# Row softmax with a relative-position bias: a sixth chunk buffer, masks built inside it, and stores that wait on a count of scaled chunks

## Chip, cores, metric

One core of one Trainium2 chip. The metric is the device time of one execution in microseconds (us), as the median of several. The other cores of the chip ran nothing of this program.

## The reference, cut to what matters

```python
B, H, S, max_rel = 2, 8, 2112, 16
logits: [B, H, S, S] float32;  rel_bias: [H, 33] float32
rel  = clip(i - j, -16, 16) + 16          # i: row, j: column
x    = logits + rel_bias[:, rel]           # the same bias for both b
out  = softmax(x, axis=-1)                 # float32
```

285.5 MB come in and 285.5 MB go out. Each element needs one addition, one exponential, one sum and one multiplication.

## The kernel before

Each of the 128 partitions owns 264 rows. They pass in 66 chunks of 4 rows (33,792 bytes per partition and chunk, 4,224 KB per transfer). SyncE issues the loads. VectorE adds the bias, which lies as one strip `F` in on-chip memory and is read at a shifted offset. ScalarE takes the exponential and the row sums; VectorE inverts the sums and scales; ScalarE issues the store. There are `BUFS` chunk buffers, and the result of chunk n is stored when chunk n+2 has had its first half added ("lag 2"; the first five stores have lag 1).

```python
R = 4; HALF = 2; BUFS = 5; NEAR = 7
qi, mm, qm, eq, lt, gt, rest = ...         # seven small mask tiles [128, 71]
L   = [const.tile([P, R*S], FP32) for u in range(BUFS)]

def store(eng, u, start):                  # ScalarE's queue
    eng.dma_start(out=rows(out, start), in_=L[u][:]).then_inc(stored[u], 16)

def reload(eng, u, start):                 # SyncE's queue
    take(eng, stored[u], 16)               # wait and count down
    load(eng, u, start)

def exps(eng, u, first):                   # ScalarE
    for s0 in range(0, R, HALF):
        take(eng, added, 1)
        if s0 == 0:
            first()                        # issues the store of an earlier chunk
        ...                                # activation with sum, twice
        e.then_inc(summed, 1)

def vec(eng, u, start, last=False):        # VectorE
    take(eng, loaded[u], 16)
    ...                                    # two additions
    ...                                    # reciprocal, scaling, twice
    if last:
        e.then_inc(scaled, 1)              # only the last store needs it
# ... (strip construction, loops over chunks: cut)
```

The softmax here doesn't subtract the row's maximum and nothing guards it: scores larger than these inputs give would overflow.

## Time and profile before

| | before |
|---|---|
| time, 3 runs | 1330.77 us (1329.46 to 1331.22) |
| the profiled execution | 1350.82 us (span 1349.0) |
| VectorE / ScalarE busy | 71% / 39% |
| DMA queues, loads + stores | 99.6% of 16 engines' span |
| moved | 571.00 MB |

Read it from the bottom: the compute engines idle a good part of the time while both DMA queues together leave nothing over. The prediction shows those lines. One part of the page that it uses without showing is the time from issue to landing (columns: tensors, issuing queue, operation, count, KB each, median us to landing):

```profile
out_dram<-L ACTq DMA_DIRECT2D x66, 4224.0 KB, 25.3
L<-in_logits_dram SPq DMA_DIRECT2D x65, 4224.0 KB, 30.4
```

A transfer needs 10.0 us of all engines and lands after 25 to 30. The rest of that time it stands in line or shares the engines with others.

### The profile page before, as it was taken

How to read it: one execution, taken by the hardware profiler on the slowest of the kernel's cores; microseconds unless marked ns; L12 is line 12 of the kernel's file. 1: busy time of each engine (PE TensorE's matmuls, PEld its weight loads, DVE VectorE, ACT ScalarE, POOL GpSimd, SP SyncE). 2: the span in 40 equal slices, each digit the busy share in tenths (PEclk: the TensorE clock that was granted, in tenths of full speed). 3: DMA queues.
4: the chain of work that ended last, by engine and by line, in shares of the span. 5: the costliest groups of instructions: out<-in, count | busy, mean ns of one | idle time of the engine just before them, and what ended most of it. 6: DMA issues, size and time to landing. Idle time of an engine off the chain costs nothing. (4 is left out here: it accounts for less than half of the span.)

```text
span 1349.0 us, 2476 instructions
## 1 busy us (share of the span) xinstructions
DVE 960.6 (71%) x539; ACT 527.1 (39%) x529; POOL 0.5 (0%) x6
## 2 busy tenths in 40 slices
DVE  5888766766766766766767767767767767767763
ACT  2444433424424424424424424434334334334332
POOL 0000000000000000000000000000000000000000
DMA  9999999999999999999999999999999999999997
GB/s 395 424 428 433 432 431 430 430 432 430 431 424 427 426 428 424 425 420 431 424 428 419 431 429 421 428 425 430 421 430 423 430 428 419 426 422 431 424 428 318
DMA packets 19587, 571.00 MB, mean 423 GB/s; under 512 B 2304, under 2 KB 2304, under 8 KB 2304
## 3 DMA queue, kind: packets, MB, share of 16 engines
q10 hardware_dynamic: 9648, 285.50, 50.1%
q1 hardware_dynamic: 9936, 285.48, 49.5%
q14 instruction: 3, 0.02, 0.0%
HBM read 285.49 MB, written 285.47 MB: 423 GB/s over the span
## 5 line engine op out<-in xcount | busy, mean ns | idle before, releaser
L120 ACT ACTIVATE L<-L 128x2112 f32<-128x2112 f32 x264 | 516.0, 1955 | 775.8 <-ACTq L86 759.6
L111 DVE TENSOR_TENSOR L<-L,F 128x4224 f32<-128x4224 f32 x132 | 595.8, 4555 | 239.2 <-DVEq L86 239.2
L134 DVE TENSOR_SCALAR L<-L,tot 128x2112 f32<-128x2112 f32 x264 | 336.5, 1317 | 21.6 <-DVEq L86 3.9
L130 DVE RECIPROCAL tot<-tot 128x2 f32<-128x2 f32 x132 | 21.9, 166 | 97.0 <-DVEq L86 97.0
L120 ACT ACTIVATION_READ_ACCUMULATOR L<-L 128x1 f32 x264 | 49.2, 186 | 0.0
L120 ACT ACT_TABLE_LOAD x1 | 1.3, 1283 | 23.1 <-ACTq L86 23.1
L178 DVE TENSOR_SCALAR rest<-lt,rbP 128x71 f32<-128x71 f32 x1 | 0.3, 257 | 7.7 <-DVEq L86 7.7
L186 DVE TENSOR_TENSOR F<-eq,rbP 128x2343 f32<-128x2343 f32 x1 | 2.6, 2600 | 0.1
L187 DVE TENSOR_TENSOR F<-F,rest 128x2343 f32<-128x2343 f32 x1 | 2.6, 2599 | 0.1
L173 DVE TENSOR_SCALAR qi<-qi 128x71 int32<-128x71 int32 x1 | 0.2, 199 | 1.5 <-DVEq L86 1.5
L181 DVE SCALAR_TENSOR_TENSOR rest<-gt,rbP,rest 128x71 f32<-128x71 f32 x1 | 0.3, 294 | 0.2 <-DVEq L86 0.2
L174 DVE TENSOR_TENSOR qm<-qi,mm 128x71 f32<-128x71 int32 x1 | 0.2, 233 | 0.1
L176 DVE TENSOR_SCALAR lt<-qm 128x71 f32<-128x71 f32 x1 | 0.2, 199 | 0.1
L176 DVE TENSOR_SCALAR eq<-qm 128x71 f32<-128x71 f32 x1 | 0.2, 198 | 0.1
L176 DVE TENSOR_SCALAR gt<-qm 128x71 f32<-128x71 f32 x1 | 0.2, 198 | 0.1
L179 DVE COPY F<-rbP 128x16 f32<-128x16 f32 x1 | 0.2, 175 | 0.1
L185 DVE COPY F<-rbP 128x16 f32<-128x16 f32 x1 | 0.2, 175 | 0.1
L210 POOL IOTA mm<- 128x71 int32 x1 | 0.2, 188 | 0.0
L207 POOL IOTA qi<- 128x71 int32 x1 | 0.2, 187 | 0.6 <-SPq L74 0.6
L265 POOL MEMSET const-bfloat16-1.0<- 128x1 bf16 x1 | 0.1, 102 | 0.0
L265 POOL MEMSET const-uint8-127<- 128x1 uint8 x1 | 0.1, 102 | 0.0
L265 POOL MEMSET const-float32-0.0<- 128x1 f32 x1 | 0.1, 99 | 0.2 <-issue 0.2
(1 smaller groups left out, 0.1 us busy)
## 6 DMA issues: line engine op xcount, KB each, us to landing
out_dram<-L ACTq DMA_DIRECT2D x66, 4224.0 KB, 25.3
L<-in_logits_dram SPq DMA_DIRECT2D x65, 4224.0 KB, 30.4
L<-in_logits_dram SPq DMA_DIRECT2D x4, 1056.0 KB, 8.9
rbP<-in_rel_bias_dram ACTq DMA_DIRECT2D x2, 8.2 KB
```

What stands on the lines that cost most here:

```text
L111: eng.tensor_tensor(out=x3, in0=x3, in1=F3, op=ALU.add).then_inc(added, 1)
L120: e = eng.activation(out=x, in_=x, func=EXP, accum_out=tot[u][:, i : i + 1])
L130: eng.reciprocal(out=t, in_=t).then_inc(inverted, 1)
L134: e = eng.tensor_scalar_mul(out=x, in0=x, scalar1=tot[u][:, i : i + 1])
L173: step(eng.tensor_single_scalar(out=qi[:], in_=qi[:], scalar=M * Q - 1, op=ALU.bitwise_and))
L174: step(eng.tensor_tensor(out=qm[:], in0=qi[:], in1=mm[:], op=ALU.subtract))
L176: step(eng.tensor_scalar(out=m[:], in0=qm[:], scalar1=0.0, scalar2=None, op0=op))
L178: step(eng.tensor_scalar(out=rest[:], in0=lt[:], scalar1=low, scalar2=None, op0=ALU.mult))
L181: eng.scalar_tensor_tensor(out=rest[:], in0=gt[:], scalar=high, in1=rest[:], op0=ALU.mult, op1=ALU.add)
L186: step(eng.tensor_tensor(out=blocks, in0=wide(eq), in1=rev, op=ALU.mult))
L187: step(eng.tensor_tensor(out=blocks, in0=blocks, in1=wide(rest), op=ALU.add))
L265: nc = _bacc.Bacc("TRN2", target_bir_lowering=False, num_devices=1)
```

## The change

The intent: one chunk more in flight, so that VectorE waits less for loads. By the prediction's accounting six buffers and the masks do not fit in the memory together, so the masks are built inside the last buffer and its first load waits until the strip is done. Every store now also takes a count that VectorE raises after scaling a chunk.

```diff
-    BUFS = 5
+    BUFS = 6
-    NEAR = 7
+    NEAR = 4
-    qi = const.tile([P, NB], INT32, tag="qi", name="qi")
-    ... six more mask tiles ...
+    qi, mm, qm, eq, lt, gt, rest = (
+        L[BUFS - 1][:, NB * m : NB * (m + 1)] for m in range(7)
+    )
     def store(eng, u, start):
+        take(eng, scaled, 1)
         eng.dma_start(out=rows(out, start), in_=L[u][:]).then_inc(stored[u], 16)
     def vec(...):
-        if last:
-            e.then_inc(scaled, 1)
+        e.then_inc(scaled, 1)
     # end of the strip's construction
+        eng.sem_inc(made, 1)
     # SyncE, first loads
             for u in range(1, BUFS):
+                if u == BUFS - 1:
+                    take(eng, made, 1)
                 load(eng, u, u * R)
```

`NEAR` is the chunk from which the looped part of ScalarE's program runs. With 4 instead of 7, the first two stores have lag 1 instead of the first five.

More of the change, by code (lines that the diff above doesn't have):

```diff
@@ L58 @@
     rbP = const.tile([P, W], FP32, tag="rbP", name="rbP")
-    qi = const.tile([P, NB], INT32, tag="qi", name="qi")
-    mm = const.tile([P, NB], INT32, tag="mm", name="mm")
-    qm = const.tile([P, NB], FP32, tag="qm", name="qm")
-    eq = const.tile([P, NB], FP32, tag="eq", name="eq")
-    lt = const.tile([P, NB], FP32, tag="lt", name="lt")
-    gt = const.tile([P, NB], FP32, tag="gt", name="gt")
-    rest = const.tile([P, NB], FP32, tag="rest", name="rest")
     L = [const.tile([P, RS], FP32, tag=f"L{u}", name=f"L{u}") for u in range(BUFS)]
     tot = [const.tile([P, R], FP32, tag=f"tot{u}", name=f"tot{u}") for u in range(BUFS)]
+    qi, mm, qm, eq, lt, gt, rest = (
+        L[BUFS - 1][:, NB * m : NB * (m + 1)] for m in range(7)
+    )
+    qi = qi.bitcast(INT32)
+    mm = mm.bitcast(INT32)
     def rows(t, start, run=RS):
@@ L79 @@
     strip = nc.alloc_semaphore("strip")
+    made = nc.alloc_semaphore("made")
     added = nc.alloc_semaphore("added")
@@ L121, in exps, with vec @@
             e.then_inc(summed, 1)
-    def vec(eng, u, start, last=False):
+    def vec(eng, u, start):
         take(eng, loaded[u], 16)
@@ L172, in strip_of @@
         take(eng, blocks_ready, 2)
-        step(eng.tensor_single_scalar(out=qi[:], in_=qi[:], scalar=M * Q - 1, op=ALU.bitwise_and))
-        step(eng.tensor_tensor(out=qm[:], in0=qi[:], in1=mm[:], op=ALU.subtract))
+        step(eng.tensor_single_scalar(out=qi, in_=qi, scalar=M * Q - 1, op=ALU.bitwise_and))
+        step(eng.tensor_tensor(out=qm, in0=qi, in1=mm, op=ALU.subtract))
         for m, op in ((eq, ALU.is_equal), (lt, ALU.is_gt), (gt, ALU.is_lt)):
-            step(eng.tensor_scalar(out=m[:], in0=qm[:], scalar1=0.0, scalar2=None, op0=op))
+            step(eng.tensor_scalar(out=m, in0=qm, scalar1=0.0, scalar2=None, op0=op))
         take(eng, table, 16 * B)
-        step(eng.tensor_scalar(out=rest[:], in0=lt[:], scalar1=low, scalar2=None, op0=ALU.mult))
+        step(eng.tensor_scalar(out=rest, in0=lt, scalar1=low, scalar2=None, op0=ALU.mult))
         step(eng.tensor_copy(out=F[:, 0:MR], in_=low.to_broadcast([P, MR])))
@@ L181, in strip_of @@
             eng.scalar_tensor_tensor(
-                out=rest[:], in0=gt[:], scalar=high, in1=rest[:], op0=ALU.mult, op1=ALU.add
+                out=rest, in0=gt, scalar=high, in1=rest, op0=ALU.mult, op1=ALU.add
             )
@@ L206, in _ @@
         def _(eng):
-            eng.iota(qi[:], pattern=[[0, NB]], base=0, channel_multiplier=M).then_inc(
+            eng.iota(qi, pattern=[[0, NB]], base=0, channel_multiplier=M).then_inc(
                 blocks_ready, 1
             )
-            eng.iota(mm[:], pattern=[[1, NB]], base=1 - M, channel_multiplier=0).then_inc(
+            eng.iota(mm, pattern=[[1, NB]], base=1 - M, channel_multiplier=0).then_inc(
                 blocks_ready, 1
@@ L241, in _ @@
             exps(eng, (N - 1) % BUFS, out_of(N - 2))
-            take(eng, scaled, 1)
             store(eng, (N - 1) % BUFS, (N - 1) * R)
@@ L248, in _ @@
             eng.wait_ge(loaded[0], 16 * R).then_inc(loaded[0], 16 - 16 * R)
-            passes(eng, 0, N - 1, lambda u, start: vec(eng, u, start))
-            vec(eng, (N - 1) % BUFS, (N - 1) * R, last=True)
+            passes(eng, 0, N, lambda u, start: vec(eng, u, start))
 _INS = ['logits', 'rel_bias']
```

## The prediction

> **What bounds the kernel now.** I read the page first, its strip of 40 slices and its DMA parts. The engines are far from full (VectorE 71%, ScalarE 39%), the DMA row is not:
>
> ```profile
> span 1349.0 us, 2476 instructions
> DVE 960.6 (71%) x539; ACT 527.1 (39%) x529; POOL 0.5 (0%) x6
> ...
> DMA  9999999999999999999999999999999999999997
> GB/s 395 424 428 433 432 431 430 430 432 430 431 424 427 426 428 424 425 420 431 424 428 419 431 429 421 428 425 430 421 430 423 430 428 419 426 422 431 424 428 318
> q10 hardware_dynamic: 9648, 285.50, 50.1%
> q1 hardware_dynamic: 9936, 285.48, 49.5%
> ```
>
> The two queues (stores 50.1%, loads 49.5%) together fill 99.6% of the time of all 16 DMA engines. The only slices under 419 GB/s are the first and the last. Next I read the waits, because a sixth buffer is an answer to waits:
>
> ```profile
> ACT L L120 <- ACTq L86: 759.6, 65, 13.1
> DVE L L111 <- DVEq L86: 239.2, 59, 4.9
> DVE tot L130 <- DVEq L86: 97.0, 131, 3.3
> ```
>
> The second line is VectorE waiting for a loaded chunk, 59 times, 239.2 / 59 = 4.1 us each. It is the sort of idle time that another buffer seems to promise back. Whether it can depends on whether the DMA engines are idle meanwhile. They are not, as stretches of the middle and both ends show (columns: stretch, length, busy time of VectorE, ScalarE, GpSimd, clock, DMA share, GB/s):
>
> ```profile
> 0.00:2.00 2.00, 0.34 (x2) 0.00 (x0) 0.53 (x6) 1.00 0.07 13
> 2.00:4.00 2.00, 0.69 (x4) 0.00 (x0) 0.00 (x0) 1.00 0.98 279
> ...
> 360.00:380.00 20.00, 14.05 (x9) 7.97 (x8) 0.00 (x0) 1.00 1.01 431
> 380.00:400.00 20.00, 13.99 (x9) 7.97 (x8) 0.00 (x0) 1.00 0.99 419
> ...
> 1330.00:1334.00 4.00, 0.00 (x0) 0.00 (x0) 0.00 (x0) 1.00 1.20 515
> 1334.00:1338.00 4.00, 0.00 (x0) 0.00 (x0) 0.00 (x0) 1.00 0.94 406
> 1338.00:1342.00 4.00, 0.00 (x0) 0.00 (x0) 0.00 (x0) 1.00 0.41 177
> 1342.00:1346.00 4.00, 0.00 (x0) 0.00 (x0) 0.00 (x0) 1.00 0.12 51
> ```
>
> The share is 1.00 throughout, in stretches of 431 and of 419 GB/s alike. So the dips are slower packets, not idle engines. The packet records say the same: nearly always 16 packets are in flight, one per engine. Of 16,768 packets of 33,792 bytes, 15,837 took 1.24 to 1.26 us (1.251 typically) and some took up to 2.5 us.
>
> **The floor.** A chunk is 128 such packets one way: 128 x 1.251 / 16 = 10.0 us. 66 chunks in and 66 out are 132 x 10.008 = 1321 us. The first chunk comes in quarters, whose 512 small packets took 11.1 us instead of 10.0, and completion writes took 1.2 us in all: 1323.4 us of pure transfer. In the profile the packets' times add up to 1343 us per engine, so about 19.5 us are slow packets. The profiled run took 1350.82 us against 1330.77 us unprofiled, 20.05 us more. I read that as: the slow packets mostly belong to profiling, and the timed run has few. Then the timed run is 1323.4 plus about 2.2 us before the first data moves, plus what is left, 1330.77 - 1325.6 = 5 us, for the last completion, unevenness between engines at the end and a few slow packets. This 5 us is all that any buffering can reach: 0.4%.
>
> **What the Trainium skill says.** "DMA: Bandwidth & Descriptors", section "Where 436 GB/s comes from", puts the ceiling of the 16 ports at 435.2 GB/s. The trace agrees: 16 x 33,792 B / 1.251 us = 432 GB/s, and the timed run averages 571.00 MB / 1330.77 us = 429 GB/s, 98.6% of the page's figure. The same section expects HBM to bind nearer 358 GB/s; here it doesn't, and the measurement decides. "SBUF — State Buffer", section "SBUF size: 192, 224, or 256?", leaves 208 KiB (212,992 B) per partition after the scratch. Six buffers of 33,792 B, the strip of 9,500 B, the table of 132 B and six sums of 16 B are 212,480 B. The seven masks (7 x 71 x 4 = 1,988 B) would not fit beside them, which is why they move into the last buffer; no run here shows the limit itself. "DMA: Bandwidth & Descriptors", section "Anatomy of one DMA — SWDGE (gpsimd) path", says that DMA engines do not wait on semaphores, and that a wait is made by the issuing sequencer. So the new waits stop SyncE's or ScalarE's queue, not a transfer already queued. In the trace the loads already queued flow while SyncE waits 1306.8 us in all.
>
> **The change part by part.**
>
> *Sixth buffer.* It removes no byte and no packet. Now a buffer's cycle is: the add starts as the load lands; the store two chunks behind is issued 4.8 us after an add starts (1211.50 to 1216.30); so a chunk's store comes 2 periods + 4.8 us after its own add. Landing times are 25.3 us for the store and 30.4 us for the reload. With a period of about 20.3 us (adds at 1211.50 and 1231.75) that is 45.4 + 25.3 + 30.4 = 101.1 us, and 5 periods are 101.5 us. So the loop is tight. But a loop can be tight because its transfers queue: 55.7 us of landing time in a period of 20.3 us means 2.7 transfers always outstanding, each needing 10.0 us of all engines. With six buffers the cycle is 6 x 20.3 = 121.8 us, so landing times grow to 121.8 - 45.4 = 76 us together and 3.8 transfers stand in line. The period remains two chunk transfers. Gain in the steady part: 0. VectorE's wait stays near 4 us a chunk, 60 times less the few chunks for which the extra buffer keeps it fed at the start (its own period when fed is 16.2 us).
>
> *Gate on the masks.* Load of buffer 5 waits for the strip, ready at 17.7 us (last strip instruction 15.13 + 2.60). Before it 5 chunks are queued, 50 us of transfer, so the queue holds until about 52 us. Cost 0.
>
> *First stores.* Stores 0 and 1 still go one chunk behind (39.9 and 56.4 us), but store 2 now goes with chunk 4 at about 88.5 us instead of 72.4. Is there enough to move till then? At 40 us, 37.6 us of the 60 us of first loads are done. Sharing evenly, store 0 ends at about 60 us and releases a reload, store 1 at about 80 us and releases another. Supply until 88.5 us: 60 + 2 x 10 + 2 x 10 = 100 us, used 86.3. Some 14 us are in hand; idle 0.
>
> *Wait on scaled chunks.* One more semaphore wait for each of 66 stores on ScalarE's queue. The store already waits for an add that VectorE runs after that chunk's scaling, so the count is there. At an estimated 0.1 us each (the gaps between dependent VectorE steps in the strip are about 0.1 to 0.15 us) it is 6.6 us on an engine that idles 775 us before activations. On the path: 0.
>
> *The end.* Last stores are issued as before: two with chunk 64, one with 65, one after the last scaling (issued 1329.15). At the last load's landing (about 1312) two to four stores are unfinished, the engines are full past 1334, and only then thin out unevenly. A store queue one deeper could hide a little of the last chunk's 16 us of compute and even out the engines: 0 to 3 us. I take 1 us.
>
> Sum: 1330.77 - 1 = about 1329.5 us.
>
> **The rivals.** (1) *The loads' wait is real latency*, and the buffer takes away VectorE's 239 us of idling, or part: even a tenth would be 24 us, 1307 us. For it: the wait is regular and the cycle is tight to 0.4 us. Against: DMA share 1.00 and a floor of 1323.4 us that is made of bytes. (2) *Deeper queues change packet speed.* Store packets took 1.251 to 1.255 us until 240 us and 1.28 to 1.30 us later, so traffic can be slower for reasons I can't see. If the timed run got the profile's whole 19.5 us of slow packets it would be 1350 us; if only a quarter, 1335. The opposite, all vanished, is about 1327. (3) *Later stores or the gate starve the start*: if my even sharing is wrong by more than 14 us, some microseconds idle, 1332 to 1340. (4) *The extra wait delays a store* in the last, exposed chunk: 0.1 us.
>
> **Range and chances.** The low end is the floor plus start and completion, about 1325; the high end allows a fifth of rival 2 or a little of rival 3, 1334. Over 2% faster would be under 1304 us, under the floor; over 2% slower would be over 1357 us and needs a starved stage or a slow mode of the memory. Chances 0.01, 0.98, 0.01.
>
> **What would show it.** Right: DMA share 1.00 and 420 to 433 GB/s in the middle, the load's and the store's landing times together near 76 us instead of 55.7, VectorE still waiting about 4 us a chunk for loads though starting some four chunks later, the first load of buffer 5 issued at about 18 us without a gap in DMA. Wrong: packets clearly faster than 1.25 us, a slice after the first under 415 GB/s, a DMA share under 0.95 between 40 and 100 us (rival 3), or store packets much slower over the whole span (rival 2).

## More of the kernel before

The wait `take(eng, added, 1)` ahead of a store of chunk n-2 already implies that chunk n-2 is scaled: VectorE's program adds chunk n only after scaling chunk n-1, and without the added wait (e6) the result is correct.

The profiled execution is 1.6% over the fastest timed one. I took that for a cost of profiling.

## The result

The changed kernel took 1332.64 us (4 runs, 1330.96 to 1333.23) against 1330.78 us of before (4 runs): ratio 1.0014, 95% interval 0.9996 to 1.0031. Ratios here and below are the mean time of one kernel's fast runs over that of the other's fast runs of the same rounds, so not quite the ratio of the medians that I quote. Executions over 1.5% slower than the fastest of the same kernel are left out of the means. The result lies inside the predicted range (1325 to 1334), and in the class "within 2%". My expected value was 1329.5.

The profile after, first its page:

```profile
span 1331.2 us, 2545 instructions
DVE 960.4 (72%) x539; ACT 522.7 (39%) x529; POOL 0.5 (0%) x6
...
GB/s 396 426 420 425 425 434 435 430 435 437 427 436 437 427 436 436 429 435 437 429 435 437 429 436 436 429 436 437 427 436 437 430 433 438 429 434 438 429 434 337
q1 hardware_dynamic: 9936, 285.48, 49.9%
q10 hardware_dynamic: 9648, 285.50, 49.8%
```

Again the queues fill 99.7% together. Bytes and packets are the same. Next the wait that the buffer was to remove (what waited, for what; us in total, times, longest), and the landing times:

```profile
DVE L L113 <- DVEq L87: 214.7, 58, 4.2
```

```profile
out_dram<-L ACTq DMA_DIRECT2D x66, 4224.0 KB, 44.6
L<-in_logits_dram SPq DMA_DIRECT2D x65, 4224.0 KB, 29.8
```

VectorE still waits 214.7 / 58 = 3.7 us a chunk. The landing times of a store and a load together went from 55.7 to 74.4 us. The new buffer holds a chunk that stands in line to be stored. Last, stretches at the start, in the middle and at the end (stretch, length, busy time of VectorE, ScalarE, GpSimd, clock, DMA share, GB/s):

```profile
0.00:2.00 2.00, 0.34 (x2) 0.00 (x0) 0.53 (x6) 1.00 0.00 0
2.00:4.00 2.00, 0.69 (x4) 0.00 (x0) 0.00 (x0) 1.00 1.02 325
360.00:380.00 20.00, 14.46 (x8) 7.82 (x9) 0.00 (x0) 1.00 1.00 433
...
1318.00:1322.00 4.00, 0.00 (x0) 0.00 (x0) 0.00 (x0) 1.00 0.96 414
1322.00:1326.00 4.00, 0.00 (x0) 0.00 (x0) 0.00 (x0) 1.00 0.39 169
1326.00:1331.00 5.00, 0.00 (x0) 0.00 (x0) 0.00 (x0) 1.00 0.08 34
```

The middle is full at 433 GB/s. At the start 2 us pass before data flows. At the end the compute engines are done at 1301 us, and the DMA engines thin out between 1322 and 1331 us: most have finished, one or two are late. These edges, and about 3 us per engine by which packets exceed their typical 1.251 us, are all that is not transfer.

### The profile page after: what moved, and what is told of

It reads as the page before. It is cut to its first block, busy times and chain, and to the rows that moved or that the text cites. A ratio compares the mean times of both kernels' runs of the same rounds, so it can differ in the third digit from the quotient of the medians.

```text
span 1331.2 us, 2545 instructions
## 1 busy us (share of the span) xinstructions
DVE 960.4 (72%) x539; ACT 522.7 (39%) x529; POOL 0.5 (0%) x6
## 5 line engine op out<-in xcount | busy, mean ns | idle before, releaser
L113 DVE TENSOR_TENSOR L<-L,F 128x4224 f32<-128x4224 f32 x132 | 595.7, 4554 | 214.7 <-DVEq L87 214.7
## 6 DMA issues: line engine op xcount, KB each, us to landing
out_dram<-L ACTq DMA_DIRECT2D x66, 4224.0 KB, 44.6
L<-in_logits_dram SPq DMA_DIRECT2D x65, 4224.0 KB, 29.8
```

The costliest lines, as they stand in the source:

```text
L113: eng.tensor_tensor(out=x3, in0=x3, in1=F3, op=ALU.add).then_inc(added, 1)
```

## The experiments

Theory: the kernel is bound by the transfer of its bytes, and what matters of the buffers is only whether enough transfers stand in line to keep 16 engines busy. Rivals: the loads' wait is real latency; six buffers help or hurt by themselves and another part of the change hides it; slow packets come from profiling or from the buffers. Kernels e1 to e4 ran on one chip, e5 to e8 on a second, e9 and e10 on that second chip in another session, and e11 and e12 on a third, each time beside the kernel before.

### e1: the kernel before, profiled again

No edit.

> The kernel before, unchanged, profiled once more. My prediction read the profile of before (1350.82 us against 1330.77 timed, about 19.5 us of slow packets) as a cost of profiling. If that is so, this profile is again near 1350 us with 15 to 20 us of slow packets. If it was the chance of that one execution, this profile is within 5 us of its timed runs, with under 6 us of slow packets, as the profile of the changed kernel was (1332.95). Rival: if five buffers as such make slow packets, the profile is again over 1340 us while kernels with six are not. Timed: ratio 1.000 within 0.002 in each case; it gives the noise of the comparison.

Measured: 1330.51 us, ratio 0.9994 (0.9973 to 1.0015). Its profile:

```profile
span 1329.4 us, 2476 instructions
...
q1 hardware_dynamic: 9936, 285.48, 49.9%
q10 hardware_dynamic: 9648, 285.50, 49.8%
```

A profiled execution is as fast as a timed one. The packet records show about 2 us of slow packets per engine (the time by which packets of 33,792 bytes exceed 1.251 us each) where the first profile had 19.5, nearly all among the loads of the first 160 us. So my reading of the 20 us as a cost of profiling is false: executions as long also come without a profile. Three of the other executions of five- and six-buffer kernels were as long or nearly (before at 1345.92 and 1352.37, e12 at 1351.80), with five and with six buffers. The first profile of before is such a slow execution. What slows the packets in them stays open. Against this second profile, the clearest difference between before and after is in the landing times: e1 has 25.7 and 28.9 us. VectorE waits 222.1 us in 59 waits there, 3.8 us each, against 3.7 in after.

### e2: the transfers alone

```diff
 # ScalarE: no exponentials
+    def copy(u, start, n=16):
+        take(eng, loaded[u], n)
+        eng.dma_start(out=rows(out, start), in_=L[u][:]).then_inc(stored[u], 16)
+    copy(0, 0, 16 * R)
+    passes(eng, 1, N, copy)
 # VectorE: the strip only
-    passes(eng, 0, N, lambda u, start: vec(eng, u, start))
```

The result is wrong: it returns the logits.

> Six buffers, same loads and stores, but no adding, no exponentials, no scaling: a store waits only for its load (wrong result on purpose). Transfer theory: the time is that of the bytes, 1323 us plus start and unevenness of the engines at the end, so 1325 to 1332 us, within 0.4% of both kernels. Rival (the loads' wait is real latency that more buffers or faster compute could win back): well below, under 1315 us. Rival (compute at the end is exposed): 1318 to 1324 us.

Measured: 1327.11 us (1326.36 to 1327.60), ratio to before 0.9971 (0.9952 to 0.9990). With no computation at all, the same transfers take 3.4 us less than the whole kernel. So removing all the compute is worth 0.3%, or 0.5% at the interval's edge. No other order of these transfers was tried, so that it bounds every arrangement is argued. The rival that promised VectorE's 239 us back is dead: the changed kernel, run again with its compute on another chip (e11), took 1327.08 us.

### e3 and e4: four and three buffers

```diff
-    BUFS = 6
+    BUFS = 4      # e3;  3 in e4
```

> The changed kernel with four buffers. With stores two chunks behind, two periods are 4.8 us plus landing of a store plus landing of a load. Transfer theory: saturation needs 40.4 us for two periods, so landing times of together 35.6 us, 1.7 transfers in line on average; that is enough or just short: 1332 to 1375 us, DMA share 0.97 to 1.00, landing times together about 36 us. Rival (a buffer's cycle is a fixed latency of about 101 us, five buffers being just enough): cycle 101 us over four buffers is 25 us a chunk, about 1670 us.

> The changed kernel with three buffers. One period is then 4.8 us plus landing of a store plus landing of a load with nothing else in line, each 10 us of transfer plus 1 to 2 us: 27 to 29 us a chunk, 1780 to 1920 us, DMA share about 0.7. Rival (fixed cycle of 101 us): 34 us a chunk, about 2220 us.

Measured: four buffers 1557.41 us (1522.87 to 1560.93; only the fastest of the four counts as fast, so no ratio is given, and the profile is of the slowest, 1560.93 us; e10 below repeats the case with fast runs), three buffers 1912.87 us, ratio 1.4372 (1.4345 to 1.4399).

Three is as expected: the cycle of a buffer leaves one period for 4.8 us plus both landings, 4.8 + 11.4 + 12.4 = 28.6 us, and the adds are 29.2 us apart (617.08 and 646.32). Four missed my range by 180 us, and the rival's 1670 missed by 113. The rule for the cycle holds, 4.8 + 21.8 + 20.7 = 47.3 us for two periods, or 23.7 us each, 66 x 23.7 = 1564 us. What fails is my assumption that 1.7 transfers in line on average keep the engines full:

```profile
q1 hardware_dynamic: 9936, 285.48, 48.3%
q10 hardware_dynamic: 9648, 285.50, 42.5%
```

```profile
640.00:650.00 10.00, 2.05 (x2) 0.00 (x0) 0.00 (x0) 1.00 1.00 433
650.00:660.00 10.00, 9.14 (x3) 4.26 (x5) 0.00 (x0) 1.00 0.77 280
660.00:670.00 10.00, 5.31 (x6) 3.63 (x4) 0.00 (x0) 1.00 0.99 426
670.00:680.00 10.00, 4.99 (x2) 0.00 (x0) 0.00 (x0) 1.00 0.70 277
```

Full stretches alternate with stretches at 0.70 to 0.77. An average in line hides that at times there is none. Overall 48.3% + 42.5% = 90.8% are busy, 9.2% idle. And the packets themselves are slower: those of 33,792 bytes add up to 1403 us per engine against 1311 us at 1.251 us each, nearly all in loads, whose packets average about 1.38 to 1.48 us after the start. 1.07 x (1 / 0.908) = 1.18, and 1557 / 1330 = 1.17.

Which load packets are slow can be read from the records. In the profiles of the five- and six-buffer kernels, the slow execution of before apart, load packets were slow only in the first 160 to 200 us at most. In e3 they were slow throughout: of the 92 us per engine by which packets exceed 1.251 us, 86 lie in load packets that started within 6 us after all engines had been empty. Run e4 shows it more plainly. Its engines were empty 126 times, about twice a chunk. The 985 load packets that started in the first microsecond afterwards averaged 1.85 us, and those that started 2 us or more afterwards 1.25 us, while the 1024 store packets of that first microsecond took 1.25 us. So running dry costs twice: the idle time, and slower loads just after it. Why the slow stretch lasts up to 6 us in e3, and one packet per engine in e4, stays open.

### e5 and e6: the wait on scaled chunks, with five buffers and without it with six

```diff
 # e5: the kernel before, and
     def store(eng, u, start):
+        take(eng, scaled, 1)
 # e6: the changed kernel, and
     def store(eng, u, start):
-        take(eng, scaled, 1)
 # with the count raised after every chunk (e5) or after the last only (e6)
```

> The kernel before with five buffers and only the wait on scaled chunks added to every store. Transfer theory: ratio to before 1.000 within 0.002 (0 us on the path); the start of an activation after a store's issue at most 0.2 us later. If the wait is what made the changed kernel 1.4 per mille slower in its first measurement, the ratio is 1.001 to 1.002 here and 1.000 in the run of six buffers without it.

> The changed kernel without the wait on scaled chunks (only the last store waits for it, as before). Transfer theory: ratio to before 0.998 to 1.003, landing of stores about 45 us and of loads about 30 us as in the changed kernel. Rival (the sixth buffer helps, and the added wait hides it): 0.99 or less.

Measured: e5 1330.92 us, ratio 1.0007 (0.9961 to 1.0053); e6 1327.88 us, ratio 0.9984 (0.9941 to 1.0028). The intervals are wide because one of the 11 runs of before, at 1345.92, still counts as fast. Neither part does anything that can be told from chance. In the traces the time from an add's start to the store's issue is 4.80 us in before (1211.50 to 1216.30) and 4.88 in after (1205.40 to 1210.28): 0.08 us more. Over all 66 stores the medians are 4.81 us in before, 4.88 in e5 and after, and 4.80 in e6, so the added wait costs 0.07 us a store, and an activation still follows the issue after 0.39 us. Landing times in e6 are 48.2 and 26.3 us, together 74.5, as with the wait.

### e7: the gate far too late

```diff
 # the end of the strip's construction
-        eng.sem_inc(made, 1)
 # VectorE
-    passes(eng, 0, N, lambda u, start: vec(eng, u, start))
+    for n in range(4):
+        vec(eng, n, n * R)
+    eng.sem_inc(made, 1)
+    passes(eng, 4, N, lambda u, start: vec(eng, u, start))
```

> The changed kernel with the load of buffer 5 held back until VectorE has scaled chunk 3 (about 84.5 us) instead of 17.7. By the bookkeeping of the prediction, 50 us of loads and 20 us of stores are all that is issued by then, done at about 73 us; 11 to 12 us of DMA idle time follow, and since transfers bound the kernel they stay: 10 to 13 us more than the changed kernel, so about 1343 us, ratio to before 1.007 to 1.011. Rival (the start has slack that the later stages make good, being bound by something else): ratio under 1.003.

Measured: 1339.19 us (1338.05 to 1340.61), ratio to before 1.0064 (1.0020 to 1.0108), 9.3 us more than the median of before and 11.3 us more than six buffers without the gate's delay in the same rounds (e6, 1327.88, which also lacks the wait on scaled chunks). The DMA engines ran dry when the bookkeeping said:

```profile
70.00:75.00 5.00, 5.00 (x2) 2.78 (x3) 0.00 (x0) 1.00 0.72 311
75.00:80.00 5.00, 4.18 (x4) 4.53 (x5) 0.00 (x0) 1.00 0.00 0
80.00:85.00 5.00, 4.02 (x4) 0.69 (x2) 0.00 (x0) 1.00 0.62 216
```

1.4 + 5.0 + 1.9 = 8.3 us of idle time. I had put it at 11 to 12 us, with the opening at 84.5 us; here the load was issued at 81.3 us, some 3 us earlier. The forecast was 10 to 13 us over the changed kernel; against e6 it is 11.3, the rest being about 2 us more of slow packets and 1 us more at the end. So this idle DMA time was not made good later, and the gate in its real place (18 to 19 us, with 50 us in line) costs nothing: the DMA engines of after are full in the stretches around it.

### e8: the first chunk in one transfer

```diff
-    for r in range(R):
-        eng.dma_start(out=L[0][:, r*S:(r+1)*S], in_=rows(logits, r, S)).then_inc(loaded[0], 16)
+    load(eng, 0, 0)
```

> The changed kernel with the first chunk loaded in one transfer instead of four quarters. Transfer theory: 512 packets of 8,448 bytes become 128 of 33,792 bytes, which took 11 us before and would take 10 us: 1 us less, ratio to the changed kernel 0.999, ratio to before 0.997 to 1.002. If the end's compute were exposed, the later start of the first chunk would cost instead: 1 to 3 us more.

Measured: 1334.60 us (1333.50 to 1336.78), ratio to before 1.0033 (0.9989 to 1.0076): not faster, and by the medians 4.7 us slower than before. This missed. One reason shows in when VectorE gets the bias table. First e8, then the changed kernel of e11 (start, us, engine, line, operation; in brackets the wait ahead of it):

```profile
27.66 0.26 DVE L179 TENSOR_SCALAR L<-L,rbP 128x71 f32<-128x71 f32 x1 [24.52 <-DVEq L87]
...
35.18 4.56 DVE L113 TENSOR_TENSOR L<-L,F 128x4224 f32<-128x4224 f32 x1 [0.68 <-DVEq L87]
```

```profile
11.06 0.26 DVE L179 TENSOR_SCALAR L<-L,rbP 128x71 f32<-128x71 f32 x1 [7.92 <-DVEq L87]
...
18.69 9.03 DVE L113 TENSOR_TENSOR L<-L,F 128x4224 f32<-128x4224 f32 x2 [0.79 <-DVEq L87]
```

The table's two small transfers share the engines with the first loads. Behind quarter packets of 8,448 bytes (about 0.34 us each) they had landed at 10.9 us, behind packets of 33,792 bytes (1.25 us) only at 27.5 us. The table's own packets fit that: from the first to the last of them 19.6 us pass in e8 and 5.1 us in e11, 3.8 times as long, and the load packets of that stretch are 3.8 times as long too (1.30 and 0.34 us). All computing starts 16.5 us later, store 2 is issued at 105.48 us, and the DMA engines run out ahead of it:

```profile
100.00:120.00 20.00, 18.24 (x10) 7.89 (x8) 0.00 (x0) 1.00 0.83 343
```

20 x 0.17 = 3.4 us idle. It agrees with the prediction's bookkeeping, which had put about 14 us in hand at this point: 16.5 - 14 is 2.5. The idle time is not the whole loss. The forecast 1 us is there in the first chunk's packets, but packets of 33,792 bytes were 4.6 us per engine over 1.251 us each in e8, and 1.0 us in e6 of the same rounds; most of that is open.

### e9 and e10: stores one chunk behind, with four and three buffers

```diff
-    BUFS = 6
+    BUFS = 4      # e9;  3 in e10
 # ScalarE, in place of the two-chunk lag
+    passes(eng, 1, N,
+        lambda u, start: exps(eng, u, lambda: store(eng, (u - 1) % BUFS, start - R)))
+    store(eng, (N - 1) % BUFS, (N - 1) * R)
```

> Four buffers, but every store goes one chunk behind instead of two. Bookkeeping: the cycle of a buffer is lag + 4.8 us + landing of store + landing of load, so three periods are 4.8 us plus the two landings, exactly as in the kernel before with five buffers and lag two. If that rule holds (buffers less lag is what counts), 1328 to 1337 us with landings of together about 55 us. If the number of buffers as such counts, about 1557 us as with four and lag two.

> Three buffers, stores one chunk behind. By the same rule it has two periods for 4.8 us plus both landings, as four buffers with lag two had (1557 us, single runs 1523 to 1561): 1500 to 1600 us. If the number of buffers as such counts, about 1913 us as with three and lag two.

Measured: e9 1336.23 us (1332.79 to 1338.39), ratio 1.0041 (1.0016 to 1.0066); e10 1554.34 us (1550.68 to 1561.15), ratio 1.1707 (1.1672 to 1.1742). Both as the rule says:

| buffers | lag | periods for 4.8 us + both landings | landings, store + load, us | time, us |
|---|---|---|---|---|
| 3 | 2 | 1 | 11.4 + 12.4 | 1912.87 (e4) |
| 3 | 1 | 2 | 21.3 + 20.6 | 1554.34 (e10) |
| 4 | 2 | 2 | 21.8 + 20.7 | 1557.41 (e3) |
| 4 | 1 | 3 | 25.3 + 28.9 | 1336.23 (e9) |
| 5 | 2 | 3 | 25.7 + 28.9 | 1330.51 (e1, the kernel before) |
| 6 | 2 | 4 | 44.6 + 29.8 | 1332.64 (the changed kernel) |

Buffers less lag is what counts. With two, the engines run dry; with three they are full; the fourth only lengthens the line. Four buffers with lag 1 come within 0.4% of five with lag 2. The 0.4% lie at the edges, where e9's strip of slices is low (354 and 410 at the start, 327 at the end):

```profile
GB/s 400 354 410 434 436 434 429 433 437 435 430 433 434 435 434 430 433 436 435 432 431 434 435 435 429 433 436 435 433 431 433 436 435 428 435 434 435 433 432 327
```

### e11 and e12: the changed kernel and e6 once more, side by side

No edit against the changed kernel (e11) and against e6 (e12).

> The changed kernel, unchanged, beside the next run on one chip. Transfer theory and chance: ratio to before 0.998 to 1.003, and within 0.003 of the ratio of the next run. If its first measurement (1.0014) told of a small real cost, 1.001 to 1.003 again.

> Six buffers without the wait on scaled chunks, once more. If the wait costs something with six buffers (this kernel was at 0.9984, the changed one at 1.0014), the changed kernel is again 3 to 5 us slower than this one in the same rounds. If that was the chance of the chip and of its few runs, the two differ by under 2 us.

Measured: e11 1327.08 us (1326.51 to 1328.35), ratio 0.9976 (0.9958 to 0.9995); e12 1331.25 us (1330.10 without its one slow run at 1351.80), ratio 1.0004 (0.9984 to 1.0024). Neither expectation of e12 held: the two differ by 3 us, over the 2 that chance was to allow, and in the other direction than a cost of the wait. Now the changed kernel is the faster of the two, and lies under before, where it had lain above. The first comparison said +0.14%, this one -0.24%, each with an interval that barely reaches or misses 1. So the interval within one chip's session is too narrow for such claims, and the change's effect is smaller than what sessions differ by, about 0.4%. The profile of e11 shows what a good execution lacks (to be read against the last three stretches of after above):

```profile
1318.00:1322.00 4.00, 0.00 (x0) 0.00 (x0) 0.00 (x0) 1.00 0.80 346
1322.00:1326.00 4.00, 0.00 (x0) 0.00 (x0) 0.00 (x0) 1.00 0.04 17
```

All engines are done soon after 1322 us. In after some still moved data at 1329. The two profiles of one and the same program differ by 6 us (1331.2 and 1325.2). By the packet records about 3.7 us of it are late engines at the end (idle time after 1300 us: 6.8 and 3.0 us) and about 2 us slower packets (3.1 and 0.9 us per engine).

## Why the prediction was right

*The bound.* Right, and now shown: without any compute the transfers take 1327.11 us (e2), inside the 1325 to 1332 that the floor of 1323.4 us plus edges gives.

*The number.* It proves little by itself: 5 of the 1330.77 us were a remainder fitted to the measured time, and the forecast is that time less 1 us. The tests of the mechanism are the landing times, the DMA share and e2.

*Gain of the sixth buffer in the steady part: 0.* Right. The sum of landing times was forecast as 76 us and is 74.4; the DMA share stays 1.00; VectorE's wait stays at 3.7 us a chunk. The tightness of the loop (101.1 of 101.5 us), which spoke for rival 1, meant a line and not a latency, as the prediction argued. I let the wait begin about four chunks later. In the profile of after it begins one chunk later (first 1.04 us at 166.73 us, in before 3.77 us at 152.25), but in the other three profiles of six buffers (e6, e11, e12) three chunks later, at 199.6 to 200.0 us. So the forecast was nearly right, and the profile of after, with slower packets at its start, hides it. From then on the extra chunk stands in the store's line, whose landing rose by 19 us, while the loads' landing stayed at 30 us.

*Gate and first stores: 0.* Right. The gate costs time only when put some 63 us too late (e7), and the spare time at store 2, forecast as 14 us, fits e8, which started 16.5 us later, 2.5 more than that, and had 3.4 us of idle time there.

*Wait on scaled chunks: 0 on the path.* Right: 0.07 us a store on ScalarE's queue (estimate: 0.1), nothing in the time (e5, e6, e12).

*The end: 1 us gained.* Not resolved. The last store is issued at 1301.53 us in after and 1309.48 in e1, so the last chunk's compute is hidden 8 us deeper. Yet the idle time after 1300 us is 3.4 and 6.2 us in two profiles of five buffers (e5, e1) and 3.0 to 6.8 us in four of six, so a gain of 1 us can't be told.

*Slow packets.* Wrong. The prediction charged 20 us of its first profile to profiling. It was a slow execution (what slowed its packets is open), and a second profile of the same kernel is as fast as a timed run. The forecast survived because it was built up from the floor of bytes and the timed runs, not from that profile's span. The rival that gave a fifth of these 20 us to deeper queues has no support: the changed kernel's packets of 33,792 bytes add up to 1314 us per engine, e1's to 1313, and e11 is faster than before. Two readings of that profile were loose as well. The stretches of 431 and 419 GB/s do not show slower packets: their packets average 1.267 and 1.279 us, 1% apart where the rates differ by 3%. The view counts a packet whole in the stretch in which it starts, which is also how 1.20 and 515 GB/s come about near the end. And the store packets slowed at about 350 us, not at 240.

My own expectation for four buffers (e3) was the one large miss. The step that failed is taking 1.7 transfers in line on average as enough: with two buffers beyond the lag the average is 1.8 (42.5 / 23.7), and still 9% is idle and packets are 7% slower.

No version was shown to beat both kernels. The run without compute leaves 0.3%, no more than sessions differ by.

## What to carry to other kernels

A wait for a load says nothing by itself: ask whether the DMA engines are idle while it lasts, and price a buffer by the number of buffers less the lag between a chunk's compute and its store. That many periods must cover both landing times (and here 4.8 us), with some transfers always in line. Build a floor from bytes and packet times, run the transfers alone once to check it, and do not take one profile for the typical execution. Where transfers bind, start-up order is worth a look: the idle DMA time of e7 and e8 was not made good.

## What the Trainium skill lacked or had wrong

- "DMA: Bandwidth & Descriptors", section "Where 436 GB/s comes from": it expects HBM near 358 GB/s to bind transfers between HBM and on-chip memory, though it also calls a measured 425 GB/s near the fabric's rate. With one core running, the runs show 433 GB/s in full stretches and 571 MB / 1327.11 us = 430 GB/s over a whole execution without compute. "HBM Reference", section "Specifications (TRN2)", says that a core streaming alone measures well above its share, about 425 GB/s, and these runs agree with that.
- No page that I found says how many transfers must stand in line to keep the engines full. Here 54.6 us of landing time per 20 us period (2.7 transfers, e1) filled them to 99.7%, and 42.5 us per 23.7 us period (1.8 transfers, e3) to 90.8%.
- Beyond latencies of a first byte and of an HBM access, no page that I found says how a packet's time depends on what ran before it: 1.251 us per 33,792 bytes in full steady streaming, 1.85 us for load packets in the first microsecond after the engines were empty (e4) and 1.25 us for store packets there, about 1.38 to 1.48 us on average for loads where the engines kept running dry (e3).
- "DMA: Bandwidth & Descriptors", section "Queues, rings and completion order", tells of a round robin between queues at packet granularity, but gives no price for a small transfer beside a large one: two transfers of 64 rows of 132 bytes landed by 10.9 us beside packets of 8,448 bytes and by 27.5 us beside packets of 33,792 bytes (e11, e8).
